# The second MLP projection as seven block products over the whole contraction instead of chunked eighths

## Chip, cores, metric

One NeuronCore of one Trainium2 chip. The metric is device time in microseconds of one execution; three runs of the kernel before gave a median of 2840.08 us (2839.7 to 2841.68). TensorE is written PE, VectorE DVE, ScalarE ACT, GpSimd POOL, SyncE SP. TensorE's clock has two levels, 1.2 and 2.4 GHz; the profile shows the granted share of the higher one.

## What is computed

One inference step of a trunk of two layers with width 1024, for 1024 prompt tokens and 8 sample tokens together (1032 columns, in the order 512 prompt, 8 sample, 512 prompt). Each layer is a token mixer and a squared-ReLU MLP; only the MLP's second half and what borders on it are touched:

```
x = x + g1 * out                                  # token mixer
h = rmsnorm(x, norm_mlp[l]) * (1.0 + s2) + sh2
x = x + g2 * (jnp.square(jax.nn.relu(h @ mlp_w1[l])) @ mlp_w2[l])
...
y = rmsnorm(x, norm_final)
```

`mlp_w1` is 1024 x 4096, `mlp_w2` is 4096 x 1024. The results have to hold float32 accuracy.

## The kernel before, in words

Everything is feature-major: a tile has 128 features in the partitions and tokens along the free dimension. TensorE works in `fp32r`, so each operand is split into a high and a low part (ACT casts `hi`, DVE subtracts to get `lo`), and `mm3` (lines 422 to 430) issues three matmuls for each pair of operands: hi·hi (L425), hi·lo (L428), lo·hi (L429).

A weight unit is a tile of 128 x 1024. `prep` (L377) makes one: a transfer on the SP queue into `raw` (two buffers), the ACT cast into `whi`, the DVE subtraction into `wlo` (three buffers each). `need` keeps units prepared up to three ahead of the one in use (`AHEAD = 3`) and takes one step of `ada_gen` (L258), which in layer 0 computes the next layer's modulation during the second projection: each step issues four transfers of 256 KB for the step after (`t<-ada`) and a group of small matmuls (L287) on the transfers of the step before. The 4 PSUM buffers `pd` of two banks each, 8 temporaries `t2` and 8 `t3` are shared by all of this.

`mlp` (L700) has two halves.

*First projection.* The 4096 x 1024 product is already done in seven half-size block products (Strassen-Winograd form): for each of 16 pairs p of row tiles (`NPAIR`), the products 1, 6, 7, 5, 2, 4, 3 of 24 matmuls with 258 columns each (`AOPS`). The two token halves have 516 columns (`HX`). DVE combines the products, and four of the seven steps finish a tile: `ff_out` (L708) applies ReLU and square on ACT, splits into hi and lo (ACT cast L616, DVE subtraction L617) and stores both parts to DRAM (`fd`) on the POOL queue. The products 1 and 2 of the last two pairs are computed early (`FRONT[1]`, before pair 12) and kept in DRAM, and right there the first chunk of the second projection's operand starts to be loaded (`load_ff(0)`).

*Second projection.* Plain: the contraction of 4096 in 8 chunks of 4 row tiles (`NCH`, `load_ff`: 8 transfers `ffc<-fd` of 516 KB a chunk on the POOL queue). For each of the 8 output row tiles m and 3 token blocks (256, 264 and 512 columns) `out_tile` (L553) accumulates 12 matmuls and DVE adds the gated result into the residual `x` (L544; L547 collects the 8 sample columns). The last chunk goes block by block (`out_last`), and the norm that follows (next layer's, or the final one) runs behind its blocks; the final norm ends the kernel with the writes of `o_y` (L1794).

The order on each engine is set by a scheduler from the written order; transfers issued by `dma_aux` (POOL) keep the written order, those by `dma` (SP) may be moved.

## Time and profile before

| | |
|---|---|
| median of 3 runs | 2840.08 us |
| the profiled execution, device time | 2840.66 us |
| its span, first to last instruction | 2838.9 us |
| mean granted clock | 0.983 |
| second projection, layer 0 | about 889 to 1279 us, the `ada` steps of layer 1 in it |
| second projection, layer 1 | about 2455 to 2827 us |
| first projection, layer 0 / layer 1 | about 540 to 889 / 2120 to 2455 us |

Busy time of an engine is a share of the span; a matmul's own duration includes its passage through the array and overlaps the next one's, so the pace of TensorE is read from the distance between starts. "Idle before, releaser" names what ended an engine's wait.

### The profile page before, as it was taken

The page shows a single profiled execution, that of the slowest core. Times are in us where ns is not written, and L with a number is a line of the kernel's source. Part 1 is how long each engine was busy: PE and PEld are TensorE (multiplying, and loading weights), DVE is VectorE, ACT ScalarE, POOL GpSimd, SP SyncE. Part 2 cuts the span into 40 slices and gives each one's busy share as a digit, 9 for nine tenths or more (in the row PEclk, how much of TensorE's full clock was granted, in tenths as well). Part 3 has the DMA queues.
Part 4 walks back from the last instruction along what each step waited for, and adds up shares of the span by engine and source line. Part 5 has one row for each costly group of instructions (what it writes and reads, how often), then busy time and mean ns, then how long its engine had stood idle before and what let it go on. Part 6 is the DMA issues. An engine that isn't in the chain of part 4 may idle for free. (4 is left out here: it accounts for less than half of the span.)

```text
span 2838.9 us, 47163 instructions
## 1 busy us (share of the span) xinstructions
PE 2726.7 (96%) x18644; PEld 2444.6 (86%) x18644; DVE 1851.9 (65%) x3723; ACT 1390.4 (49%) x2351; POOL 223.2 (8%) x384
## 2 busy tenths in 40 slices
PE   6999999989999999999899999999999999999997
PEld 4889888889998888888789897787789999899996
DVE  5666444797665333357788888998779767544446
ACT  5775411565563000027686766878667556300102
POOL 0000000121113101000000000000002111300100
PEclk8999999999999999999999999999999999999999
DMA  8332333366459666514645545543436654944431
GB/s 297 81 100 65 102 119 120 101 201 206 143 155 347 233 215 235 186 53 87 160 143 131 182 127 141 148 130 112 116 123 190 205 163 142 331 153 143 164 109 63
DMA packets 193581, 441.60 MB, mean 156 GB/s; under 512 B 31377, under 2 KB 49169, under 8 KB 193361
## 3 DMA queue, kind: packets, MB, share of 16 engines
q1 hardware_dynamic: 129808, 269.25, 31.9%
q0 software_dynamic: 63552, 169.34, 18.0%
q8 instruction: 147, 2.41, 0.4%
q14 instruction: 74, 0.60, 0.1%
HBM read 340.44 MB, written 98.08 MB: 154 GB/s over the span
## 5 line engine op out<-in xcount | busy, mean ns | idle before, releaser
L407 ACT CAST whi<-raw 128x1024 fp32r<-128x1024 f32 x220 | 229.9, 1046 | 820.4 <-PE pd L428 584.6
L425 PE MATMUL pg<-hh,whi 128*128 128x256 f32 (+2 forms) x1616 | 537.6, 333 | 11.1 <-ACT hh L525 5.7
L428 PE MATMUL pg<-hl,whi 128*128 128x256 f32 (+2 forms) x1616 | 525.2, 325 | 1.9 <-DVE hl L526 1.9
L429 PE MATMUL pg<-hh,wlo 128*128 128x256 f32 (+2 forms) x1616 | 524.3, 324 | 0.0
L425 PE MATMUL pd<-ffc,whi 128*128 128x256 f32 (+2 forms) x1488 | 479.2, 322 | 3.3 <-DVE x L544 2.4
L544 DVE SCALAR_TENSOR_TENSOR x<-pd,mod,x 128x256 f32<-128x256 f32 (+1 forms) x384 | 219.2, 572 | 399.7 <-PE pd L429 395.0
L429 PE MATMUL pd<-ffc,wlo 128*128 128x256 f32 (+2 forms) x1488 | 477.4, 321 | 0.0
L428 PE MATMUL pd<-ffc,whi 128*128 128x256 f32 (+2 forms) x1488 | 476.2, 320 | 0.0
L408 DVE TENSOR_TENSOR wlo<-raw,whi 128x1024 fp32r<-128x1024 f32 x220 | 269.0, 1224 | 160.1 <-ACT whi L407 149.2
L425 PEld LDWEIGHTS pg<-hh,whi 128*128 128x128 f32 x1616 | 310.0, 192 | 48.7 <-issue 7.6
L428 PEld LDWEIGHTS pg<-hl,whi 128*128 128x128 f32 x1616 | 310.3, 192 | 31.0 <-issue 5.5
L429 PEld LDWEIGHTS pg<-hh,wlo 128*128 128x128 f32 x1616 | 309.5, 192 | 24.5 <-issue 0.7
L425 PEld LDWEIGHTS pd<-ffc,whi 128*128 128x128 f32 x1488 | 280.4, 188 | 44.0 <-ACT whi L407 15.9
L425 PE MATMUL pd<-hh,whi 128*128 128x258 f32 x1024 | 294.1, 287 | 15.8 <-ACT t L781 4.4
L429 PEld LDWEIGHTS pd<-ffc,wlo 128*128 128x128 f32 x1488 | 279.9, 188 | 22.6
L428 PEld LDWEIGHTS pd<-ffc,whi 128*128 128x128 f32 x1488 | 279.9, 188 | 21.8 <-issue 0.2
L428 PE MATMUL pd<-hh,whi 128*128 128x258 f32 x1024 | 292.1, 285 | 0.7 <-DVE hh L617 0.7
L429 PE MATMUL pd<-hh,wlo 128*128 128x258 f32 x1024 | 290.5, 284 | 0.0
L425 PEld LDWEIGHTS pd<-hh,whi 128*128 128x128 f32 x1024 | 196.2, 192 | 19.5 <-issue 6.1
L428 PEld LDWEIGHTS pd<-hh,whi 128*128 128x128 f32 x1024 | 195.9, 191 | 1.8 <-DVE hh L617 1.3
L429 PEld LDWEIGHTS pd<-hh,wlo 128*128 128x128 f32 x1024 | 196.0, 191 | 0.0
L425 PE MATMUL pg<-ffh,whi 128*128 128x264 f32 (+2 forms) x544 | 176.9, 325 | 1.1 <-ACT bcz L1478 0.7
(319 smaller groups left out, 5458.5 us busy)
## 6 DMA issues: line engine op xcount, KB each, us to landing
raw<-W SPq DMA_DIRECT2D x307, 512.0 KB, 4.2
ffc<-fd POOLq DMA_DIRECT2D x128, 516.0 KB, 11.2
fd<-x POOLq DMA_DIRECT2D x100, 516.0 KB, 4.4
t<-ada SPq DMA_DIRECT2D x192, 256.0 KB, 5.5
t<-csd SPq DMA_DIRECT2D x64, 256.0 KB, 4.7
fd<-t POOLq DMA_DIRECT2D x56, 258.0 KB, 4.6
x<-xd POOLq DMA_DIRECT2D x16, 516.0 KB, 10.6
t<-st_ss SPq DMA_DIRECT2D x32, 256.0 KB, 4.4
```

The costliest lines, as they stand in the source:

```text
L407: S.copy(hi, raw)
L408: V.tensor_sub(lo, raw, hi.bitcast(F32))
L425: mm = PE.matmul(pt, wh, xh, start=first and i == 0, stop=False)
L428: PE.matmul(pt, wh, xl, start=False, stop=False)
L429: PE.matmul(pt, wl, xh, start=False, stop=last and i == n - 1)
L544: V.scalar_tensor_tensor(x[:, m, s:s + npr], pt[:, :npr], mod[:, self.gi + m, 0:1], x[:, m, s:s + npr], op0=ALU.mult, op1=ALU.add)
```

## The change

The second projection is done in seven half-size products too, over the whole contraction: outputs in two halves of 4 row tiles (m = 0 to 3), contraction in two halves, tokens in two halves of 516. The four blocks of the squared-ReLU activations are B11, B12, B21, B22, and T1 = B12 - B11, T3 = B22 - B12, T2 = T3 + B11, T4 = B21 - T2. Products in the order 2, 1, 5, 6, 7, 3, 4, with the right operands B21, B11, T1, T2, T3, B22, T4.

- **First projection**: `ff_out` no longer splits. ACT squares into one of 8 slots in the upper half of tile `X`; DVE forms T3, T2, T1 and T4 there; seven tiles of 258 KB a pair are stored in float32 (`td`) where there were four pairs of hi and lo.
- **Right operands**: `load_op` loads half an operand (8 row tiles, four transfers, 2.1 MB) into the `lo` tile and splits it in place, in four pieces of 2 x 516 columns (`split_op`), into three sets of buffers that take turns. The first half operand is loaded at the old place of `load_ff(0)`, the second before the last product of pair 15.
- **Weights**: products 2, 1 and 4 use units as stored. Products 5, 6 and 7, 3 need sums: for each of their 8 units two transfers of 256 KB bring the first summand (a unit, or the sum stored earlier), one of 512 KB the second, DVE adds or subtracts (2 x 512 columns), and the sums of 5 and 6 are stored to DRAM (`sd`) two units later for 6 and 3.
- **Products**: a unit serves 2 output row tiles x 4 contraction tiles x 2 column halves x 3 = 48 matmuls of 258 columns; 8 units a product. Product 4 runs in two column halves of 8 units with 24 matmuls each, and so loads its units twice. A product's result is added to one to four tiles of `x` (`BOUT`: 1, 4, 2, 3, 2, 1, 1 for 2, 1, 5, 6, 7, 3, 4).
- The residual `x` is two tiles of 4 rows (`Two`), reloaded at once; the sample columns are kept aside (`xs`) and added before the last column half of product 4. The following norm is spread by hand over products 3 and 4 (`to_odd`, `to_out`); its last block has 258 columns (before: 256).

```diff
+BPROD = (2, 1, 5, 6, 7, 3, 4)
+BOPS = [(i, hb, q, mp) for i in range(7) for hb in (range(2) if i == 6 else (None,))
+        for q, mp in (BSEQ if i else BFIRST)]
+BSET = [(0, 1), (2, 0), (1, 2), (0, 1), (2, 0), (1, 2), (0, 1)]
...
+            while sums and sums[0][0] <= idx - 2:
+                _, d, h = sums.pop(0)
+                for j in range(2):
+                    dma(d[:, 512 * j:512 * j + 512], h[j])
+            pr = BPROD[i]
+            if pr in (5, 6, 7, 3):
...
+                h = [t2(512), t3(512)]
+                for j in range(2):
+                    dma(h[j], a[:, 512 * j:512 * j + 512])
+                raw = load_unit(*second)
+                for j in range(2):
...
+                        V.tensor_sub(h[j], h[j], raw[:, c])
+                    S.copy(hi[:, c], h[j])
+                    V.tensor_sub(lo[:, c], h[j], hi[:, c].bitcast(F32))
...
-                hi, lo = (M["X"][:, k, i * HX:i * HX + HX] for i in range(2))
-                split_to(hi, lo, r)
-                dma_aux(fd[m][:, :, half * HX:half * HX + HX], v2(M["X"][:, k]))
+            d = slot(p, i)
+            S.activation(d, r, AF.Square)
+            if q != 2:
+                store({5: "B21", 4: "B22", 3: "B11"}[q], p, d)
+            if q == 4:
+                V.tensor_sub(slot(p, 3), d, slot(p, 1))
+                store("T3", p, slot(p, 3))
+            elif q == 3:
+                t1, t2_, t4 = slot(p, 1), slot(p, 5), slot(p, 6)
+                V.tensor_add(t2_, slot(p, 3), d)
+                V.tensor_sub(t1, t1, d)
+                V.tensor_sub(t4, slot(p, 0), t2_)
...
+            for c in range(0, KT, 2):
+                dma_aux(lo[:, c:c + 2].bitcast(F32), d[:, c:c + 2])
...
-                        for b in range(3):
-                            out_tile(ws(m), srcs, res, m, b)
-                            bg.tick()
+            for m in (2 * mp, 2 * mp + 1):
+                if q == qs[0]:
+                    pts[m] = pd()
+                pt = pts[m]
+                for b in range(2) if hb is None else (hb,):
+                    c = slice(b * hw, b * hw + hw)
+                    mm3(pt[:, b, 0:hw], [(hi[:, o:o + P], lo[:, o:o + P], rh[:, k, c], rl[:, k, c])
+                                         for k, o in ((q % 2 * 4 + k, 256 * k + m % 2 * P) for k in range(4))],
+                        q == qs[0], q == qs[-1])
+                if q == qs[-1]:
+                    for o, th in BOUT[BPROD[i]]:
...
+                            V.scalar_tensor_tensor(xv, pt[:, :, 0:hw], gate, xv, op0=ALU.mult, op1=ALU.add)
```

The SP queue during the second projection of layer 0, where the `ada` transfers run (`raw<-W` is a weight unit, `t` are temporaries). Before:

```order
L202 DMA raw<-W 128x1024
L202 DMA t_11825<-ada 128x512
L202 DMA t_11826<-ada 128x512
L202 DMA t_11827<-ada 128x512
L202 DMA raw<-W 128x1024
L202 DMA t_11828<-ada 128x512
L202 DMA t_11930<-ada 128x512
L202 DMA t_11929<-ada 128x512
L202 DMA t_11931<-ada 128x512
```

Four `ada` transfers stand between two weight units, and each of those units feeds 72 matmuls. With the change, in product 6:

```order
L217 DMA sd<-t_10680 128x512
L217 DMA sd<-t_10681 128x512
L217 DMA t_10850<-sd 128x512
L217 DMA t_10851<-sd 128x512
L217 DMA raw<-W 128x1024
L217 DMA t_10921<-ada 128x512
L217 DMA t_10922<-ada 128x512
L217 DMA t_10923<-ada 128x512
L217 DMA t_10924<-ada 128x512
L217 DMA sd<-t_10757 128x512
L217 DMA sd<-t_10758 128x512
```

Now nine transfers go with each unit, and a unit feeds 48 matmuls; the sums stored here are those of two units earlier.

DVE in the second projection of layer 0. Before, with L544 the addition into `x`, L547 the sample columns and L408 the split of a weight unit:

```order
L408 TENSOR_TENSOR wlo<-raw,whi 128x1024
L544 SCALAR_TENSOR_TENSOR x<-pd,mod,x 128x256 x2
L547 TENSOR_TENSOR racc<-pd,racc 128x8
L544 SCALAR_TENSOR_TENSOR x<-pd,mod,x 128x512
L544 SCALAR_TENSOR_TENSOR x<-pd,mod,x 128x256 x2
L547 TENSOR_TENSOR racc<-pd,racc 128x8
L544 SCALAR_TENSOR_TENSOR x<-pd,mod,x 128x512
```

With the change, at the end of product 6 and in product 7 (L452 forms a weight sum, L454 splits it, L837 splits a piece of the right operand, L953 adds into `x`):

```order
L452 TENSOR_TENSOR t_11260<-t_11260,raw 128x512
L452 TENSOR_TENSOR t_11261<-t_11261,raw 128x512
L837 TENSOR_TENSOR rr<-rr 128x2x516
L454 TENSOR_TENSOR wlo<-t_11260,whi 128x512
L454 TENSOR_TENSOR wlo<-t_11261,whi 128x512
L837 TENSOR_TENSOR rr<-rr 128x2x516 x3
L953 SCALAR_TENSOR_TENSOR x<-pd,mod,x 128x516
L452 TENSOR_TENSOR t_11344<-t_11344,raw 128x512
L452 TENSOR_TENSOR t_11345<-t_11345,raw 128x512
L960 TENSOR_TENSOR racc<-pd,racc 128x4
```

Four operations a unit where there was one, and additions into `x` queue behind operations that need a transfer (`raw`).

The POOL queue at the end of layer 1's first projection, with the change (pairs 13 to 15; `b_` and `kept` are tiles of pairs 14 and 15 put aside earlier):

```order
L223 DMA td<-x 128x516 x7
L223 DMA t_25691<-kept 128x516
L223 DMA x<-b_25115 128x516
L223 DMA td<-x 128x516 x7
L223 DMA x<-b_25181 128x516
L223 DMA td<-x 128x516 x3
L223 DMA rr<-td 128x2x516 x4
L223 DMA td<-x 128x516 x4
L223 DMA x<-xd 128x1032 x8
```

The eight loads of the residual and the half operand of product 1 that follow them start only when the last four tiles of pair 15 have been stored.

## Rows read from the trace of the kernel before

**Rows 1.** The page's busy times of the engines over the span.

```profile
PE 2726.7 (96%) x18644; PEld 2444.6 (86%) x18644; DVE 1851.9 (65%) x3723; ACT 1390.4 (49%) x2351; POOL 223.2 (8%) x384
```

**Rows 2.** Stretches of 50 us: the stretch and its length, busy us (and instructions) of PE, weight loads (PEld), DVE, ACT and POOL, granted clock, busy share of the DMA engines, GB/s. The first two lie in layer 1's first projection, the third in the mixer before it, the last two in layer 1's second projection.

```profile
2250.00:2300.00 50.00, 50.00 (x420) 50.00 (x419) 36.88 (x61) 27.37 (x46) 7.89 (x12) 1.00 0.60 181
2300.00:2350.00 50.00, 50.00 (x418) 49.80 (x417) 33.57 (x54) 27.50 (x47) 6.06 (x9) 1.00 0.43 130
...
1850.00:1900.00 50.00, 50.00 (x254) 40.92 (x253) 47.70 (x97) 37.98 (x59) 1.43 (x2) 1.00 0.37 120
...
2500.00:2550.00 50.00, 50.00 (x319) 45.10 (x318) 21.09 (x41) 5.27 (x5) 2.09 (x5) 1.00 0.17 48
2600.00:2650.00 50.00, 50.00 (x317) 45.01 (x316) 19.92 (x39) 4.34 (x5) 5.90 (x12) 1.00 0.49 166
```

**Rows 3.** The PE timeline, start and duration in us: two neighbouring matmuls of 512 and of 256 columns in the second projection, and of 258 in the first.

```profile
2601.67 0.40 PE L425 MATMUL pd<-ffc,whi 128*128 128x512 f32 x1
2601.91 0.40 PE L428 MATMUL pd<-ffc,whi 128*128 128x512 f32 x1
...
2604.48 0.28 PE L425 MATMUL pd<-ffc,whi 128*128 128x256 f32 x1
2604.60 0.28 PE L428 MATMUL pd<-ffc,whi 128*128 128x256 f32 x1
...
745.18 0.28 PE L425 MATMUL pd<-hh,whi 128*128 128x258 f32 x1
745.30 0.28 PE L428 MATMUL pd<-hh,whi 128*128 128x258 f32 x1
```

**Rows 4.** The chain of work that ended last, start and duration: the same matmul of a 512-column group in two successive output row tiles (36 matmuls apart).

```profile
2467.15 0.24 PE pd L428
2472.83 0.24 PE pd L428
```

**Rows 5.** Groups by line, engine, operation and shape (count, busy us, mean ns, idle before): layer 1's second projection (the first four), its first projection (the others).

```profile
L544 DVE SCALAR_TENSOR_TENSOR x<-pd,mod,x 128x512 f32<-128x512 f32 x64 | 48.1, 751 | 130.4 <-PE pd L429 130.4
L408 DVE TENSOR_TENSOR wlo<-raw,whi 128x1024 fp32r<-128x1024 f32 x28 | 34.3, 1225 | 2.9
L407 ACT CAST whi<-raw 128x1024 fp32r<-128x1024 f32 x28 | 29.5, 1055 | 279.6 <-PE pd L428 279.6
L547 DVE TENSOR_TENSOR racc<-pd,racc 128x8 f32<-128x8 f32 x56 | 8.7, 156 | 0.0
...
L403 DVE TENSOR_TENSOR wlo<-t,whi 128x512 fp32r<-128x512 f32 x44 | 29.2, 686 | 0.0
L617 DVE TENSOR_TENSOR x<-t,x 128x516 fp32r<-128x516 f32 x40 | 27.8, 695 | 24.7 <-ACT x L616 24.7
L616 ACT CAST x<-t 128x516 fp32r<-128x516 f32 x41 | 25.6, 625 | 1.3
```

**Rows 6.** Stretches around the place where the first chunk of the second projection's operand is loaded, in layer 0 and layer 1, and one in the first chunks of layer 0's second projection (columns as in the stretches above).

```profile
860.00:880.00 20.00, 15.98 (x107) 15.39 (x106) 11.98 (x19) 8.49 (x15) 4.80 (x8) 0.83 1.06 349
2430.00:2445.00 15.00, 11.05 (x65) 10.37 (x64) 9.40 (x15) 5.76 (x10) 3.43 (x6) 0.77 1.16 378
...
870.00:875.00 5.00, 3.75 (x17) 3.55 (x18) 4.71 (x8) 4.10 (x7) 0.54 (x1) 0.61 1.27 387
900.00:905.00 5.00, 5.00 (x35) 4.58 (x34) 1.98 (x2) 1.06 (x1) 1.12 (x3) 1.00 1.14 387
910.00:915.00 5.00, 5.00 (x33) 4.45 (x32) 2.23 (x5) 1.05 (x1) 1.44 (x3) 1.00 1.04 414
```

**Rows 7.** DMA issues by line (count, KB each, median us from issue to landing): two from layer 1's second projection (2500 to 2750 us), two from 850 to 885 us, one from 900 to 965 us, where the DMA engines are full.

```profile
raw<-W SPq DMA_DIRECT2D x22, 512.0 KB, 3.8
ffc<-fd POOLq DMA_DIRECT2D x40, 516.0 KB, 9.4
...
fd<-x POOLq DMA_DIRECT2D x6, 516.0 KB, 11.0
raw<-W SPq DMA_DIRECT2D x4, 512.0 KB, 6.4
...
raw<-W SPq DMA_DIRECT2D x6, 512.0 KB, 10.5
```

**Rows 8.** The PE timeline in layer 0's second projection: one `ada` step (8 records in one row) and the matmul after it.

```profile
1010.07 1.06 PE L287 MATMUL pd<-t,ct 128*32 128x512 f32 x8
1011.06 0.39 PE L425 MATMUL pd<-ffc,whi 128*128 128x256 f32 x1
```

**Rows 9.** The end of the kernel: a stretch with the last output tiles and the norm behind them, the last matmul of the projection, the norm's own matmul, and the last multiplications by the norm on DVE.

```profile
2797.00:2827.00 30.00, 25.71 (x198) 24.18 (x196) 24.71 (x73) 10.59 (x24) 0.00 (x0) 1.00 0.25 93
...
2826.61 0.28 PE L429 MATMUL pd<-ffc,wx 128*128 128x256 f32 x1
2828.96 0.70 PE L461 MATMUL pd<-t,ones 128*128 128x256 f32 x2 [2.07 <-DVE t L493]
...
2832.30 2.07 DVE L1794 SCALAR_TENSOR_TENSOR x<-x,nf,t 128x256 f32<-128x256 f32 x5
```

More of the change, by code (lines that the diff above doesn't have):

```diff
@@ L824, in mlp @@
+            bg.tick(2)
+        x = new_x()
+        for m in range(KT):
+            dma_aux(x[:, m, :], xd[:, m])
+        load_op(1, 0)
+        acc = tp.tile([P, KT, NS], F32, name="racc", tag="racc", bufs=2)
+        V.memset(acc, 0.0)
+        fin = finish()
+        pts = {}
+        hw = HX // 2
+        for n, (i, hb, q, mp) in enumerate(BOPS):
+            j = n % 8
+            hi, lo = need(f"b{l}", n)
+            if n == 8 and more:
                 ada[0] = more()
-            elif c == NCH - 1:
+            elif i == 6 and hb == 0 and j == 0:
```

331 lines of the change are left out of this document (227 added, 104 removed).

## Prediction, made before the changed kernel ran

> **What bounds the kernel now.** Read the busy times first [rows 1]: PE is busy for 96% of the span, DVE for 65%. Since a PE record overlaps the next, the second look is at stretches of 50 us [rows 2]: in both projections of layer 1 PE never stops, with DVE at 20 to 37 of 50 us, the granted clock at 1.00 and the DMA engines at 0.17 to 0.60. So the two projections run at the pace of the matmuls, and the third look is at what sets that pace. Two starts of 512 columns lie 0.24 us apart, two of 256 or 258 columns 0.12 us [rows 3]. Half the columns, half the time: the price goes by columns and hardly by the matmul. Averaged over many: an output row tile of 36 matmuls (12 each of 256, 264 and 512 columns) repeats after 5.68 us [rows 4], and 838 matmuls of 258 columns took 100 us [rows 2], 0.1193 us each.
>
> **The sum** is made against the profiled execution, 2840.66 us (span 2838.9 and 1.8 around it), 0.6 above the median of the three runs. About 0.2%, 5.7 us, is what a measurement can tell from no change.
>
> *1. Matmuls.* Before, a layer's second projection is 8 chunks x 8 output row tiles = 64 groups of 5.68 us [rows 4]: 363.5 us. After, 7 products x 8 units x 48 = 2688 matmuls of 258 columns, where there were 2304 wider ones: 2688 x 0.1193 = 320.7 us [rows 2]. More instructions, fewer columns: 42.8 us less a layer, **-85.6 us** in both. The `ada` steps of layer 0, 24 of about 1.0 us [rows 8], stay.
>
> *2. First projection.* Each pair loses four ACT casts of 0.625 us and four DVE subtractions of 0.695 us and gets four DVE operations of the same width [rows 5]. PE is full there while ACT has 27 and DVE 37 of 50 us [rows 2]: 0. Cover gone would mean DVE at 50 of 50.
>
> *3. The burst before pair 12.* Before, 4.2 MB of operand are loaded between the stores there, at 349 to 378 GB/s, and PE loses time: 107 matmuls in 20 us and 65 in 15 us [rows 6], where the steady pace gives 8.4 a us, so 168 and 126 [rows 2]. That is 61 x 0.1193 = 7.3 us in each layer, partly because the clock falls to 0.61 after the pause [rows 6], a mixture of 1.2 and 2.4 GHz. The change loads 2.1 MB there. I take half of the loss back: **-7 us** (0 to -14.5).
>
> *4. Start of the second projection.* The first four units of product 2 need only the half operand loaded early, and last 4 x 48 x 0.1193 = 22.9 us. In that time come the second half (2.1 MB), the residual (4.2 MB) and half an operand of product 1 (2.1 MB): 8.4 MB at about 400 GB/s [rows 6] is 21 us, but the residual waits for the last stores of pair 15. Before, a similar load was borne at a full PE, in the stretches from 900 us [rows 6]. **+3 us** (0 to +10).
>
> *5. Products 5 and 6 in layer 0.* This is the place I trust least. A unit keeps PE for 48 x 0.1193 + 1.0 = 6.7 us, and asks for 1.05 MB of `ada`, 0.52 MB of first summand, 0.52 MB of second, 0.52 MB of sum to store, and its eighth of the right operand, 0.53 MB: 3.15 MB. The full DMA engines moved 387 to 414 GB/s [rows 6], so 3.15 MB take 7.6 to 8.1 us: the transfers, not PE, set the pace. There is also a chain on SP: an `ada` transfer needs a temporary whose sum was stored one unit before, so SP stands until that store has landed, and the next unit's loads stand behind it. I take 8.0 us a unit: 16 x 1.3 = 20 us, less about 6 for the one unit that weights are ahead, plus 3 for clock falls like those at the burst [rows 6]: **+17 us**. Below: 0, if fewer transfers coincide. Above: 10.5 us a unit, the landing time of a weight unit when the engines are full [rows 7], which gives 16 x 3.8 = 60 us.
> The Trainium skill, "DMA: Bandwidth & Descriptors", section "Where 436 GB/s comes from", says that for transfers between HBM and SBUF the HBM side binds at about 358 GB/s for a core. By that figure a unit would take an estimated 8.8 us and the term would be about 30 us; the rows here show 387 to 414 GB/s over 5 us and up, so I stay with the rows.
>
> *6. Products 5 and 6 in layer 1* have no `ada`: 2.10 MB a unit, 5.2 us at 400 GB/s against 5.73 us of PE. Just hidden; weight sums can be formed up to five units ahead there. **+3 us** (0 to +10). DVE is closest to full in product 6: 16 tile-wide sums (8 units of 2 adds) and 16 splits at 0.69, 8 operand splits at 1.24 (by width from L408), 12 additions into `x` at 0.75 and 12 small ones at 0.16 come to 42.9 of 45.8 us [rows 5]. The mixer shows DVE at 47.70 of 50 us under a full PE [rows 2], so I price that at 0; without that cover it would be queued behind `raw`.
>
> *7. Product 4* takes 16 units of 24 matmuls, 2.86 us each. A `raw` buffer is held for landing 3.8 us [rows 7], cast 1.05 and subtraction 1.23 [rows 5], 6.1 us; two buffers give a unit every 3.05 us at best. 16 x 0.2 = 3 us are late. In layer 1 the final norm comes on top: DVE sums to about 46 of 45.8 us, and before, such a stretch with DVE at 24.71 of 30 us held PE at 25.71 [rows 9]. **+3 and +6 us** (0 to +8 each).
>
> *8. The end.* From the last matmul at 2826.6 us over the last addition, square, norm matmul and eight multiplications to the end is 12.2 us [rows 9]; the last block now has 258 columns instead of 256 and the same steps: 0 (2 either way).
>
> Sum: 2840.7 - 85.6 - 7 + 3 + 17 + 3 + 9 = **2780 us**, 2.1% faster.
>
> **The rivals.**
> *A. All transfers hide.* Terms 5 and 6 vanish and the burst's loss comes back wholly: 2780 - 20 - 7.5 = 2752 us. For it: the layer 1 engines have room [rows 2], and 8 + 8 temporaries let loads run ahead. Against: 3.15 MB in 6.7 us is more than any row moved.
> *B. Layer 0 runs at landing time,* 10.5 us a unit: +60 instead of +17, 2823 us. For it: stores of 11.0 us and weight units of 10.5 us in full stretches [rows 7], and nine transfers a unit on one queue. Against: those medians belong to queues that were filled by far more than a unit's transfers.
> *C. Slower: the store-to-load chain paces products 5 and 6 in both layers.* If the round trip of a sum (stored, landed, its buffer refilled, the next unit's summand landed) is 10.5 us in layer 1 as well [rows 7], the terms 5 and 6 become 16 x 3.8 + 16 x 4.8 = 136 us instead of 20: 2896 us. It decides from the point where 16 x (T - 6.7) + 16 x (T - 5.73) eats the 80.6 us that the other terms leave, at T = 8.7 us a unit in both layers. Against: in layer 1 the SP queue waits for no `ada`, and 2.1 MB in 8.7 us is 241 GB/s, which the engines exceed easily; stores and loads of neighbouring units are independent.
> *D. The pace goes by weight load, not by column.* There is one weight load a matmul, and in the first projection PEld is busy 50.00 of 50.00 us [rows 2]. Were the 0.12 us the load's, the 384 additional matmuls a layer would cost 2 x 384 x 0.119 = 91 us instead of saving: 2932 us. Against: in the second projection, with half the matmuls at 512 columns costing 0.24 us [rows 3], PEld has gaps (45 of 50) [rows 2] and PE none, so columns bind.
> The Trainium skill's page "TensorE: Matmul & The Clock Gate", section "Back-to-back issue gap", gives for sustained pairs of load and matmul about 81 ns at 128 columns and 131 ns at 512, so that wide matmuls are much cheaper a column; by it, as an estimate, the change would be about 12 us slower a layer. The rows show 0.24 us at 512 columns, twice that at 256, so this case does not bear it out.
>
> **How the numbers follow.** Forecast (2765 to 2800): 0.60. A: 0.18. B, and between it and the forecast: 0.13. C, any mixture that passes its point: 0.05. D: 0.01. Stalls that just cancel the gain: 0.03. Faster 0.60 + 0.18 + 0.13 = 0.91; same 0.03; slower 0.06. The range reaches from A's time to B's: 2752 to 2823; C, D, the cancelling case and a part of A's lower side lie outside, under 0.2.
>
> **What would show it.** Term 1: matmuls of 258 columns at 0.119 us, a product without stalls in 45.8 us, a second projection of layer 1 near 330 us where it was 372. Term 3: the stretch before pair 12 with more than 107 matmuls in 20 us. Term 5: units of about 8 us in products 5 and 6 of layer 0, PE waiting for `ada` or for a weight sum, DMA share at 1 and above 380 GB/s. Term 6: PE full in the same products of layer 1. Term 7: PE with gaps of a few tenths in product 4, ended by the cast or the subtraction. It is wrong if PE stalls in products 1, 2 or 3, if layer 1's products 5 and 6 stall as much as layer 0's, or if DVE, not DMA, ends the waits.

## The result, and the profile of the changed kernel

The changed kernel takes 2819.57 us (median of four runs, 2814.00 to 2825.63), the kernel before on the same chip 2839.89: ratio 0.9928, 95% interval 0.9907 to 0.9950. The profiled execution took 2820.48 us (span 2818.7). The interval is clear of 1, and the gain is 0.7%. The forecast was 2780: the sign held, the size did not. Of 60 us forecast, 20 came.

The page's busy times, which answer to [rows 1], its two rows on the splits of the operand, and its two rows on the DMA issues that matter below:

```profile
PE 2662.7 (94%) x19442; PEld 2453.6 (87%) x19442; DVE 1995.6 (71%) x3800; ACT 1496.6 (53%) x2477; POOL 277.9 (10%) x476
...
L836 ACT CAST rr<-rr 128x1032 fp32r<-128x1032 f32 x112 | 117.3, 1056 | 156.5 <-DMA rr<-td 156.4
L837 DVE TENSOR_TENSOR rr<-rr 128x1032 fp32r<-128x1032 f32 x112 | 135.5, 1227 | 64.4 <-ACT rr L836 64.1
...
raw<-W SPq DMA_DIRECT2D x371, 512.0 KB, 4.3
...
rr<-td POOLq DMA_DIRECT2D x112, 516.0 KB, 8.4
```

PE was busy for 96% and is for 94% of a shorter span: it now waits. ScalarE stands 156 us before the operand's splits, for the operand to land; whether that costs anything is looked at below.

Stretches of the changed kernel (columns as in [rows 2]): layer 0's products 5 and 6, then in layer 1 the end of product 2, product 5, the border from product 6 to 7, and the end:

```profile
990.00:1050.00 60.00, 54.71 (x444) 48.05 (x444) 37.08 (x66) 17.38 (x25) 6.99 (x11) 1.00 1.01 368
1050.00:1110.00 60.00, 56.62 (x448) 49.52 (x441) 34.99 (x58) 15.84 (x23) 3.67 (x7) 0.97 1.03 390
...
2455.00:2505.00 50.00, 46.77 (x366) 46.35 (x365) 27.46 (x32) 20.55 (x21) 17.50 (x28) 0.93 0.91 340
...
2550.00:2590.00 40.00, 40.00 (x337) 40.00 (x336) 32.47 (x57) 12.77 (x20) 3.10 (x5) 1.00 0.97 340
...
2640.00:2670.00 30.00, 21.94 (x153) 21.53 (x152) 19.48 (x33) 10.71 (x15) 2.82 (x4) 0.83 0.72 256
...
2777.00:2807.00 30.00, 28.07 (x208) 28.02 (x209) 15.39 (x34) 10.46 (x22) 0.00 (x0) 0.89 0.42 125
```

Product 5 of layer 1 runs full: the 337 matmuls in its 40 us include those cut by the ends of the stretch, and by the starts a unit of 48 takes 5.75 us, 0.1198 us each. At the border to product 7 it is 153 in 30 us where some 250 would fit.

By stages (from the first to the last matmul of each): first projections 347.1 -> 344.6 and 335.1 -> 342.8 us, second projections 396.0 -> 383.8 and 371.0 -> 358.5, the mixer between them 835.7 in both, the end 12.3 -> 11.5. (Layer 0's second projection of before ends at 1285 us, not at 1279 as the table of stages has it.) So each second projection won 12 us where the matmuls alone give 42.8.

What a product takes beyond its matmuls (45.8 us), beyond the busy time of `ada`'s and, in product 4, beyond that of the norm's own products (L520, 1.0 to 2.7 us), from the starts of every 48th matmul (24th in product 4), in us. The 1.0 of product 1 in layer 0 is `ada`'s too: its steps are busy for 1.07 us each, but lengthen a unit by 1.2 us, from 5.75 to 6.94.

```
                   layer 0                             layer 1
product         2    1    5    6    7    3    4     2    1    5    6    7    3    4
the change     3.7  1.0  6.8  6.0  4.1  0.2 12.9   6.7  0.2  0.2  4.3 12.2  0.2 12.5
late_rstd      2.8  1.0  7.0  6.1  6.1  0.2  5.9   6.5  0.2  0.2  4.9 13.2  0.2  6.5
rawsums        4.8  1.0  1.2  0.9  0.5  0.2 12.8   0.2  0.2  0.2  0.2  0.2  0.2 12.9
quarter_op     4.6  1.0  3.2  0.9  2.1  0.2 11.1   4.8  0.2  2.0  0.2  0.2  0.2 10.7
nostore        3.6  1.0  9.6 10.6  1.9  1.8 12.7   4.1  0.2  0.2  0.2 10.8  0.2 12.6
no_ada         4.1  0.2  0.2  3.6 12.2  0.2 12.3   4.0  0.2  0.2  3.7 13.2  0.2 12.1
late_pin       7.1  1.0  6.1  4.8  1.5  0.2  8.5   9.0  0.2  1.7  8.7  0.2  0.2  6.2
late_paced_pin 7.5  1.0  2.5  7.7  1.0  0.2  8.6   9.2  0.2  0.2  0.8  8.4  0.2  6.2
```

Two places carry most of it: product 4, and the borders of products 5 to 7.

**Product 4.** PE's waits in layer 1's second projection (us in total, times, longest), PE's timeline in layer 0, and the stretch of 10 us around it:

```profile
PE pd L488 <- DVE wlo L454: 10.5, 3, 4.0
PE pd L602 <- ACT sm L599: 4.9, 1, 4.9
PE pd L520 <- DVE t L552: 2.4, 1, 2.4
PE pd L484 <- ACT whi L463: 2.3, 1, 2.3
```

```profile
1241.73 1.45 PE L602 MATMUL pd<-sm,ones 128*128 128x8 f32 x6 [4.93 <-ACT sm L599]
```

```profile
1236.00:1246.00 10.00, 5.07 (x27) 4.86 (x26) 6.01 (x13) 3.36 (x9) 0.00 (x0) 0.67 0.50 159
```

L602 are the sixteen ones products of `sample_rstd`, eight columns wide (the view ends after six). They stand in PE's queue right behind the first half of product 4, and wait for that half's own eviction, gated sum, add to `x` and squares. PE stops 4.9 us, the granted clock of the 10 us around is 0.67 (a mixture of 1.2 and 2.4 GHz), the sixteen products take 3.6 us, and the unit takes 11.4 us where 2.9 are matmuls.

**The border of products 6 and 7.** VectorE in layer 1 (L452 and L450 form weight sums, L454 splits one into `wlo`), ScalarE's cast of product 7's first weight sum, PE where it goes on, and the POOL queue's operand transfers:

```profile
2643.18 1.29 DVE L452 TENSOR_TENSOR t<-t,raw 128x512 f32<-128x512 f32 x2 [6.26 <-issue]
2645.70 1.29 DVE L452 TENSOR_TENSOR t<-t,raw 128x512 f32<-128x512 f32 x2 [1.22 <-DMA raw<-W]
2646.91 1.29 DVE L454 TENSOR_TENSOR wlo<-t,whi 128x512 fp32r<-128x512 f32 x2
2650.01 1.29 DVE L452 TENSOR_TENSOR t<-t,raw 128x512 f32<-128x512 f32 x2 [1.82 <-issue]
2655.60 0.69 DVE L450 TENSOR_TENSOR t<-raw,t 128x512 f32<-128x512 f32 x1 [4.29 <-DMA t<-sd]
```

```profile
2631.72 1.14 ACT L453 CAST whi<-t 128x512 fp32r<-128x512 f32 x2 [4.62 <-PE pd L487]
```

```profile
2647.64 0.58 PE L488 MATMUL pd<-rr,wlo 128*128 128x258 f32 x1 [4.04 <-DVE wlo L454]
```

```profile
2631.99 2.82 POOL L223 DMA_DIRECT2D rr<-td  x4 [35.71 <-PE pd L488]
2643.56 2.11 POOL L223 DMA_DIRECT2D rr<-td  x3 [8.76 <-PE pd L488]
```

The landing time of a weight tile issued right behind the first burst, at 2635.75 us:

```profile
DMA to landing us min/median/max: 9.8/9.8/9.8
```

Both half operands of a product, 2.1 MB each, go out within 15 us (the view ends at the third transfer of the second). The weight tile issued behind the first takes 9.8 us to land, where the page's median is 4.3. VectorE stands 6.26 us before a sum (the trace names no releaser; the sum's `raw`, issued at 2634.54, has no landing on record) and 1.22 us before the next, for the tile above. Counted from the first unit of product 5, two sums, two casts and two splits a unit, these are the sums of product 7's units 5 and 6, needed 29 us later and more. Behind them in VectorE's queue stands the split of product 7's first unit, whose cast was done at 2632.9: PE stops 4.0 us for it. The second unit's split, cast by 2641.3, starts at 2659.1, behind the sum at 2655.60, which belongs to product 3 and waits 4.3 us for a stored sum. So what stops PE is not that its own weights land late, but that VectorE's queue holds a sum for a unit far ahead, whose transfer is late, in front of the split that PE needs next. PE's three waits of this kind come to 10.5 us (L454 above); after the first the matmuls start 0.21 us apart for 4 us, with a granted clock of 0.57 from 2645 to 2650 us.

In layer 0's products 5 to 7 PE waits for evictions and for `ada`'s loads; below, VectorE and PE at the border from product 5 to 6:

```profile
PE pd L484 <- DVE racc L960: 8.8, 4, 3.2
PE pd L316 <- DMA t<-ada: 3.0, 4, 1.9
```

```profile
1054.79 1.29 DVE L452 TENSOR_TENSOR t<-t,raw 128x512 f32<-128x512 f32 x2 [2.75 <-DMA raw<-W]
1056.00 0.15 DVE L960 TENSOR_TENSOR racc<-pd,racc 128x4 f32<-128x4 f32 x1
```

```profile
1057.03 0.36 PE L484 MATMUL pd<-rr,whi 128*128 128x258 f32 x1 [3.15 <-DVE racc L960]
```

In this longest of the four, too, a sum that waits for `raw` stands in VectorE's queue ahead of what PE needs, here the eviction that frees a PSUM buffer.

### The profile page after: what moved, and what is told of

The parts are those of the page before. It is cut to its first block, busy times and chain, and to the rows that moved or that the text cites. A ratio compares the mean times of both kernels' runs of the same rounds, so it can differ in the third digit from the quotient of the medians.

```text
span 2818.7 us, 49673 instructions
## 1 busy us (share of the span) xinstructions
PE 2662.7 (94%) x19442; PEld 2453.6 (87%) x19442; DVE 1995.6 (71%) x3800; ACT 1496.6 (53%) x2477; POOL 277.9 (10%) x476
## 5 line engine op out<-in xcount | busy, mean ns | idle before, releaser
L484 PE MATMUL pd<-rr,whi 128*128 128x258 f32 x1792 | 516.3, 288 | 11.7 <-DVE racc L960 8.8
L488 PE MATMUL pd<-rr,wlo 128*128 128x258 f32 x1792 | 512.4, 286 | 13.4 <-DVE wlo L454 10.5
L487 PE MATMUL pd<-rr,whi 128*128 128x258 f32 x1792 | 511.2, 285 | 0.0
L484 PEld LDWEIGHTS pd<-rr,whi 128*128 128x128 f32 x1792 | 344.5, 192 | 32.1 <-issue 26.0
L488 PEld LDWEIGHTS pd<-rr,wlo 128*128 128x128 f32 x1792 | 344.4, 192 | 16.3 <-DVE wlo L454 11.1
L487 PEld LDWEIGHTS pd<-rr,whi 128*128 128x128 f32 x1792 | 344.2, 192 | 0.5 <-issue 0.5
L484 PE MATMUL pd<-hh,whi 128*128 128x258 f32 x1024 | 294.9, 288 | 21.6 <-ACT whi L424 10.6
L836 ACT CAST rr<-rr 128x1032 fp32r<-128x1032 f32 x112 | 117.3, 1056 | 156.5 <-DMA rr<-td 156.4
L837 DVE TENSOR_TENSOR rr<-rr 128x1032 fp32r<-128x1032 f32 x112 | 135.5, 1227 | 64.4 <-ACT rr L836 64.1
```

The lines of the kernel that those rows point to most:

```text
L484: mm = PE.matmul(pt, wh, xh, start=first and i == 0, stop=False)
L487: PE.matmul(pt, wh, xl, start=False, stop=False)
L488: PE.matmul(pt, wl, xh, start=False, stop=last and i == n - 1)
L836: S.copy(hi[:, c:c + 2], src)
L837: V.tensor_sub(lo[:, c:c + 2], src, hi[:, c:c + 2].bitcast(F32))
```

## The experiments

Chips differ (before ran at 2836 to 2856 us beside these), so ratios to before are compared; the change has 0.9928.

**late_rstd.** The samples' ones products three units later:

```
-        yield                      (to_odd, ahead of sample_rstd)
+        yield  x4
-        r8 = sample_rstd(sm(NS))   (to_out: moved into the writes of n1, m == 1; the rows ys at m == 2)
```


> The squares' sum of the samples (the ones products of sample_rstd) is formed three units later, in the second half of product 4, in both layers; nothing else moves. Theory: in the profile of the change PE stands 5.1 us in each layer before those ones products (the two gaps put down to ACT sm L599), because they stand in PE's queue behind the last unit of the first half and wait for that unit's own eviction, the gated sum, the add to x and the squares. With the clock fall after it the last unit of the first half took 11.4 and 9.7 us where 2.9 are matmuls, and the next one 5.0 and 6.4. Both units then fall below 5 us, and 10 to 16 us come back in all: about 2807 us. Rival 1: the stop only moves with the products (the chain behind them is late there too): a gap of 4 to 5 us in the second half of product 4, and 2816 to 2822 us. Rival 2: it is won in product 4 and lost again where the samples' columns are then late (start of the odd mixer, output of the samples): the second projection shortens and the stretch after it grows by as much.


Measured 2802.95 us, 0.9888 (0.9870 to 0.9905): the last unit of the first half takes 2.9 us in both layers (11.4 and 9.7), the lost time in product 4 goes from 12.9 and 12.5 to 5.9 and 6.5. The theory holds for the place, and of PE's waits the one for L602 is gone. The trace has 9 us of the gain in the second projections; the rest lies in stages that the edit does not touch, and in which traces of different runs differ by as much.

**late_norms.** The other ones products of product 4 later too:

```
+yield  x2      (ahead of nm.rstd in to_odd and of n0.rstd in to_out)
+yield          (ahead of n1.rstd in to_out; the writes of the output bunched by two)
```


> late_rstd, and the ones products of the other norms that stand in PE's queue during product 4 later as well: those of the 512 columns two units later in both layers, those of the 254 columns in layer 1 one unit later; the writes of the output are bunched by two to end in the same unit. Theory: they too wait in PE's queue for evictions, squares and adds that are only just done (in late_rstd the second unit of product 4 took 7.8 and 8.2 us, and three units of the second half 4.5 to 4.6, where 2.9 are matmuls): 4 to 5 us of each layer's first half and 3 us of layer 1's second half come back beyond late_rstd, about 2792 us. Rival: the chain of squares and adds on ScalarE and VectorE is itself behind, so the wait only moves on with the products: 2799 to 2804 us.


Measured 0.9885 (0.9869 to 0.9901), no more than late_rstd. The wait of the first half went (0.0 and 1.4 us lost there), but the second half now loses 3.5 and 4.9: most of it moved on, as the rival has it.

**spread_op, spread_both, late_spread2.** The transfers of the operands one in a unit:

```
-    dma_aux(lo[:, c:c + 2].bitcast(F32), d[:, c:c + 2])
+    later.append((lo[:, c:c + 2].bitcast(F32), d[:, c:c + 2]))
+    if later: dma_aux(*later.pop(0))                  (at the end of each unit)
```


> The first half operand of a later product (load_op(i + 2, 0)) still begins to load after the last unit of a product, but its four transfers of 516 KB go out one in a unit over four units instead of four at once; each is still loaded two units or more before it is split. Theory: the stops at the borders of the products come from the two half operands, eight transfers of 516 KB in 11.5 us on the POOL queue, which fill the DMA engines while raw<-W and t<-sd wait behind them (9.7 to 9.8 us to landing at 2634 to 2637 us of the change's profile). In layer 1 products 6 and 7 took 50.1 and 58.0 us where 45.8 are matmuls, in layer 0 the first units of products 5, 6 and 7 took 9.4, 12.0 and 10.3. By this 10 to 16 us of layer 1 and 5 to 10 us of layer 0 come back: about 2800 us, and the landing of raw<-W in that stretch falls to 5 us or less. Rival: the weight sums are late by their own chain (DVE in program order, SP's queue, two raw buffers), whatever else is on the DMA engines: units 0 and 1 of product 7 in layer 1 stay over 9 us, and the time within 4 us of 2820.

> Both half operands of a product go out spread, one transfer of 516 KB in each unit: the one that was issued at once after unit 5 in units 5, 6, 7 and 0, the one after unit 7 in units 1 to 4 of the next product, each split later by a unit where its load moved. In spread_op only the second burst was spread. Theory: in layer 1 raw<-W and t<-W that were issued at 2635.75 to 2637.1 us, right behind the first burst (2632.0 to 2634.1), landed after 9.7 to 9.8 us with the DMA engines full, and the sums of the next two units were late by that; a weight tile then never stands behind more than one operand transfer and lands in 6 us or less. Products 6 and 7 lose 5 us or less together in layer 1 (16.5 in the change) and products 5 to 7 8 us or less in layer 0 (17): 18 to 22 us, 0.986 of before. Rival: the same bytes in the same product keep the DMA engines full whatever the order, or the sums' chain on VectorE is late anyhow; the first two units of product 7 keep over 16 us together, and the ratio stays at 0.991 to 0.994.

> late_rstd and spread_both together. Theory: the two lie in different products (4 there, 5 to 7 here), so their gains add: 0.9888 times what spread_both gives against the change's 0.9928, 0.982 if that is 0.986. Rival: what the first gives back is taken by the second (the odd mixer or the output then waits for something else): no better than the better of the two.


Measured 0.9934 (0.9920 to 0.9949), 0.9963 (0.9950 to 0.9976), 0.9901 (0.9886 to 0.9916): none is faster than its counterpart without the edit. They say nothing on the burst, since it was still there. POOL in spread_both:

```profile
2637.47 2.83 POOL L223 DMA_DIRECT2D rr<-td  x4 [35.19 <-PE pd L488]
```

Four in 2.8 us, as in the change, although the program has them in four different units: POOL's queue waits once, for the last matmul on the buffer, and then sends all four, so a later place in the program changes nothing.

**rawsums, quarter_op, nostore.** Three kernels that leave transfers out, and so do not compute the whole reference.

```
rawsums:     both terms of a sum from the one raw tile; no dma(h[j], ...), no store of sums
quarter_op:  dma_aux(lo[:, 0:2]...) alone; src = lo[:, 0:2] for all four parts
nostore:     a = A["W"][...] also in products 6 and 3; sums.append(...) left out
```


> In products 5, 6, 7 and 3 the two terms of each weight sum are taken from the one raw tile that is loaded anyway, so the transfers of the first term, the stores of the sums of products 5 and 6 and their loads in 7 and 3 are left out (what is summed is then not what the kernel needs); VectorE and ScalarE do the same work. Theory: what is lost in these products (17 us over the matmuls in layer 0, 16.5 in layer 1) is lost to transfers, three of 256 KB beside each 512 KB of weights: 25 to 33 us come back, about 2790 us, and products 5, 6, 7 and 3 take 45.8 to 48 us each (in layer 0 with 7 to 8 of ada matmuls more). Rival (VectorE's own queue): the adds, subtractions and evictions are the pace; then products 6 and 7 of layer 1 keep 50 and 58 us and the time stays over 2812.

> Of each half operand only the first of four transfers is made, and all four parts are split from it (the operands are then not those the kernel needs); every other instruction stays, the transfers of the weight sums too. Theory: the stops at the product borders need the operands' bursts, 2.1 MB each; at a quarter of that products 6 and 7 of layer 1 take 46 to 48 us each (50.1 and 58.0) and layer 0's products 5 to 7 lose 5 us or less (17), product 2's last units too: 26 to 35 us, 0.981 to 0.984 of before. Rival: the extra load per unit of the sums and its wait on SP and VectorE make the stops, as nostore left open; then over 8 us stay at the border of products 6 and 7, and the ratio over 0.989.

> The sums of products 5 and 6 are not stored, and products 6 and 3 load a weight tile where they loaded a stored sum (the sums are then not those the kernel needs). The loads into half tiles, VectorE's and ScalarE's work and SP's order of loads stay; a unit of products 5 and 6 moves 1.0 MB in place of 1.5. Theory (how much moves in a row): products 6 and 7 of layer 1 fall to 46 to 48 us (50.1 and 58.0 now), and layer 0's 5 to 7 lose 3 to 9 us in place of 17: 20 to 27 us, about 2796 us. Rival (the extra load and its wait in SP's queue and on VectorE): the stops at the border of products 6 and 7 stay at over 8 us in both layers, 2810 us or more.


Measured 2777.63 us, 0.9793 (0.9778 to 0.9808); 2785.35 us, 0.9793 (0.9776 to 0.9810); 0.9929 (0.9914 to 0.9944). Products 6 and 7 of layer 1 in the change, in rawsums and in quarter_op:

```profile
2592.00:2702.00 110.00, 99.48 (x786) 98.86 (x785) 76.30 (x126) 37.32 (x55) 11.69 (x17) 0.94 0.79 283
```

```profile
2560.00:2655.00 95.00, 95.00 (x795) 95.00 (x794) 78.40 (x129) 39.10 (x55) 12.24 (x18) 1.00 0.54 186
```

```profile
2567.00:2662.00 95.00, 95.00 (x796) 95.00 (x795) 76.57 (x127) 35.52 (x52) 3.56 (x5) 1.00 0.68 233
```

With most of the operand's bytes or with the sums' transfers away PE is full, with VectorE busy for 77 to 78 of 95 us: the amount of VectorE's work is not the pace. Without the stores alone most of the loss stays (in layer 1's products 6 and 7 10.8 us of 16.5, all in product 7; in layer 0's products 5 to 7 22 us where it was 17), although they are a third of a unit's weight bytes in products 5 and 6. So what counts is not bytes alone, but that loads which a sum waits for are late.

**no_ada.**

```
-mlp(0, mi(0, 5), to_odd, more=lambda: ada_gen(1, ...))
+V.memset(mod[:, 48:96], 0.25); mlp(0, mi(0, 5), to_odd)
```


> The modulation of layer 1 is not computed in the second projection of layer 0 but set to a constant: its matmuls (24.4 us of TensorE by the rows of before), its 6 MB a group of loads and the PSUM tile that it holds are left out. Theory: in layer 0 the held PSUM tile and its loads cost more than the matmuls: the stops that end with an eviction (racc L960, 9.5 us in products 5 to 7) go, so 30 to 40 us come off and layer 0's products 5 to 7 look as layer 1's: about 2785 us. Rival: ada costs only its matmuls, and the stops at the borders of the products stay: 24 us, 2796 us, with the first units of products 5, 6 and 7 still over 9 us.


Measured 2787.96 us, 0.9823 (0.9805 to 0.9841); layer 0's second projection is 29.3 us shorter than the change's, of which 28.6 are `ada`'s 24 steps of 1.19 us. Layer 0 then looks as layer 1 does (3.6 and 12.2 us lost in products 6 and 7), and PE's waits in these products now end with the split L454 (10.7 us), no longer with evictions. Products 5 to 7 lose 16.0 us without `ada`, 16.9 with it: the loss moved, from 12.8 us in products 5 and 6 to 3.8 there and 12.2 in product 7. So the rival, by the sum: `ada` costs its matmuls, and without it stops of the same size come in another place.

**order251.**

```
-BPROD = (2, 1, 5, 6, 7, 3, 4)
+BPROD = (2, 5, 1, 6, 7, 3, 4)
```


> One line: the products of the second projection run in the order 2, 5, 1, 6, 7, 3, 4 (before 2, 1, 5, 6, 7, 3, 4), so that product 1, whose units load 512 KB, stands between 5 and 6, whose units move three times that (raw, the other term or a sum, and the store of a sum). Theory after spread_op and rawsums: what stops products 6 and 7 is the transfers that 5 and 6 need in a row, 1.5 MB in 5.75 us beside the operands' 4.2 MB in 46 us, some 360 GB/s for 92 us, which uses up what the weights were ahead; split by a light product it does not build up. In layer 1 the 4.3 and 12.2 us lost in products 6 and 7 fall to 4 or less together, in layer 0 the 17 lost in 5, 6 and 7 to 8 to 12: 17 to 21 us, about 2800 us. Rival: it is the chain of a sum itself (stored in 5, loaded in 6, stored in 6, loaded in 3; SP's queue in order) and not how much moves: the first two units of product 7 keep over 20 us together, and the time stays over 2812.


Measured 0.9934 (0.9921 to 0.9947). Neither forecast: the stops moved. 13.8 us in layer 0 and 7.3 in layer 1 are lost in product 5, now second; in layer 1 5.9 us stay in product 7. Setting a light product between 5 and 6 does not take the loss away.

**raw3.**

```
-N2, N3E, N3O, N3M = 8, 14, 6, 8
+N2, N3E, N3O, N3M = 8, 14, 6, 6
+if ph.nr % 3 == 0: pool, tag, n = ph.pool, "rawx", 1       (load_unit, in the MLPs)
```


> In both MLPs a third raw tile of weights; to make room, six t3 tiles in place of eight. Theory: the stops in the first projection (7.3 us in layer 1 at 2158, 2213, 2243 and 2275 us, about as much in layer 0, and 5.5 us in each before pair 12) come from the loop of two raw tiles: a load starts when the tile before last has been summed, and takes 4.7 us and up to 6.3. With a third one 8 to 12 us come back in the first projections, and the second projections lose less at the borders: about 2805 us. Rival: with the loads earlier the same bytes only collide earlier (the DMA engines are at 0.6 of their time there and full in the bursts), or the t3 tiles that were given up stop the sums: within 4 us of 2820, or slower.


Measured 0.9930 (0.9917 to 0.9942). Layer 1's first projection took 334.4 us (342.8), layer 0's 346.7 (344.6); layer 1's products 6, 7 and 3 lost 24 us (16.7 in the change). One edit with two sides, in no place clear; a third raw tile did not take the stops away.

**paced, late_paced, late_paced_fp, paced1, late_paced1.** Ahead of each operand transfer GpSimd copies one column of a weight tile, so that POOL's queue cannot run ahead:

```
+ nc.gpsimd.tensor_copy(pace[:, 0:1], units[wpos[0] + 2][1][:, 0:1])    (paced1: + 1)
  dma_aux(*later.pop(0))
```


> spread_both, and ahead of each operand transfer one column of the weight tile that was split last is copied on GpSimd, so that POOL's queue sends the transfer only when that tile is there: one transfer of 516 KB per unit, behind the weights of the units ahead. Theory (burst): raw<-W and t<-W never stand behind more than one operand transfer, land in 6 us or less in products 5 to 7, and 2 to 6 us are lost there in layer 1 (16.5 in the change) and 4 to 10 in layer 0 (17): 18 us or more less than the change, 0.984 to 0.987 of before. Rival (sum of bytes: 2.0 MB in 5.75 us in products 5 and 6 is what the DMA engines move at best): the stops stay over 10 us in each layer, wherever they fall, or operands come late as new stops at units 2 and 3: 0.990 to 0.996.

> late_rstd and paced together. Theory: the gains lie in different products and add: about 0.9888 times paced's ratio over 0.9928, 0.981 if paced gives 0.985. Rival: no better than the better of the two.

> late_paced, and the first half operand of product 2, whose four transfers go out at once before pair 12 in the first projection, paced too: one in every two products of pair 12. Theory: that burst is what stops TensorE before pair 12 (5.45 us at 862.1 and 5.51 at 2423.6 us in the change, after ScalarE's split of a weight tile that landed late): the stop falls below 2 us in both layers, and 7 to 10 us come back beyond late_paced. Rival: the stop is made by the sixteen weight rows of pairs 14 and 15 themselves, which need one load per product where others need none: it stays within 1 us of 5.5, as before the change too.

> paced, each operand transfer gated by the weight tile of one unit earlier, so that it goes out some 5.75 us sooner: in paced the split of the operand on ScalarE waited for the transfer 154 us in 27 places of layer 1, one unit's time each, and the weights' splits stood behind it. Theory (burst): these waits go to under 1 us each, raw<-W still lands in 8 us or less, and products 5 to 7 lose 4 to 8 us in each layer where the change loses 17: 0.985 to 0.988 of before. Rival (sum of bytes): with the waits of paced gone the stops at the borders are back as in the change: over 12 us in each layer, 0.991 to 0.996; third case: the gates and the operands are still in each other's way, slower than before.

> late_rstd and paced1 together. Theory: the gains add, 0.996 times the ratio of paced1, so 0.981 to 0.984 if the burst is the cause; rival: no better than late_rstd's 0.9888.


Measured 1.0377 (1.0358 to 1.0396), 1.0336 (1.0320 to 1.0351), 1.0338 (1.0324 to 1.0352), 1.0321 (1.0304 to 1.0338), 1.0283 (1.0269 to 1.0298): all slower, the third case of paced1. The first two waits of `paced` from 2560 to 2800 us (`pace` is the gate), then ScalarE's waits in products 5 to 7 of paced1's layer 1, and of the change's:

```profile
ACT rr L839 <- DMA rr<-td: 154.2, 27, 10.9
POOL pace L977 <- DVE wlo L454: 152.7, 22, 10.0
```

```profile
ACT rr L839 <- DMA rr<-td: 134.6, 25, 8.7
```

```profile
ACT whi L453 <- PE pd L487: 51.2, 11, 8.3
ACT rr L836 <- DMA rr<-td: 37.6, 19, 6.3
```

ScalarE's queue holds the splits of operands ahead of weights' splits, in an order made by the scheduler and not written in the code. A gate then waits for a weight split that stands behind the split of an operand not yet sent, and so the transfers come late: in paced1 they go out 8 us apart on the average from 2615 to 2657 us, where a unit's matmuls take 5.75. The last row shows that in the change, too, ScalarE stands 38 us there for operands, with weights' splits behind it. But none of PE's stops there ends with a cast (all three end with VectorE's L454), so in the change this wait is not what stops PE.

In late_paced_fp the gates in the first projection held nothing: the four transfers went out at 852.50, 853.34, 854.74 and 856.69 us, and each gate took 0.2 us without a wait.

**late_pin and late_paced_pin.** The splits of both kinds held in the written order, without and with paced1's gates, both with late_rstd's edit:

```
-S.copy(hi[:, c:c + 2], src)
+tc.keep_in_program_order(S.copy(hi[:, c:c + 2], src))      (and each sum and split of prep and load_op)
```


> late_rstd, with the splits of weights and operands in the second projection held in the order in which the code writes them on ScalarE and VectorE (the sums of a unit's two halves ahead of their splits). Theory: the order changes what waits for what a little, not the bytes: products 6 and 7 of layer 1 together still lose 12 to 20 us and the ratio is that of late_rstd, 0.987 to 0.991. Rival: the order in which the scheduler bunched the operands' splits is itself the cause of the stops: under 8 us lost there, 0.984 or less.

> late_pin with paced1's transfers: one operand transfer per unit, gated by a weight tile, and the splits in an order in which no gate stands behind the split that waits for it. Theory (burst): products 5 to 7 lose 4 to 8 us in each layer (16 to 19 in late_rstd), ScalarE waits under 20 us in all for operands in layer 1, 0.981 to 0.985. Rival (sum of bytes, two raw tiles): over 12 us are lost in each layer although the longest landing of raw<-W is under 8 us, 0.987 or more. Third case: the gates still delay the operands, slower than late_pin.


Measured on one chip: 2830.93 us, 0.9914 (0.9898 to 0.9929), and 2817.48, 0.9865 (0.9850 to 0.9880). ScalarE's waits in the same products of late_pin:

```profile
ACT whi L458 <- PE pd L494: 41.9, 13, 4.6
ACT whi L458 <- DVE t L455: 31.0, 6, 8.7
ACT whi L458 <- DVE t L451: 19.9, 5, 6.2
```

PE's waits in late_pin there:

```profile
PE pd L491 <- ACT rr L843: 4.4, 1, 4.4
PE pd L494 <- DVE rr L844: 1.8, 2, 0.9
```

ScalarE has no wait for an operand left, and PE none for a weight's split or an eviction; in late_rstd its waits for the split L454 came to 12.4 us there. So the order did make those stops. In their place PE waits for the operand's own splits (L843, L844; in layer 0 one of 3.4 us). Products 5 to 7 lose 12.4 and 10.6 us (19.2 and 18.3 in late_rstd), between the forecasts of theory and rival. But product 2 loses 4.3 and 2.5 more, and as a whole late_pin is not faster than late_rstd.

late_paced_pin beats late_pin by 13 us by the medians, with intervals apart, and against late_paced1, which has the same gates without the fixed order, it is 4.1% lower. It also has spread_both's later loads and splits of a half operand, so the 13 us are those of gate and spread together. Its own forecasts both missed: 11.2 and 9.4 us are lost in products 5 to 7, and the longest landing of a weight tile in layer 1's is 9.1 us (11.0 in late_pin). The profiled runs show only 1.2 us less than late_pin in products 5 to 7 of each layer; they were late_pin's fastest and late_paced_pin's slowest, so where the rest lies stays open. late_paced_pin has the lowest ratio of all kernels that compute the whole reference; against late_rstd, on another chip, the intervals overlap.

## Why the prediction was wrong

The step that failed first is in term 6: VectorE was priced at 0 because its busy time fits (42.9 of 45.8 us), and product 7 got no term at all. What counts is not how busy VectorE is but what stands in its queue: sums that wait for a late `raw` in front of the splits that PE needs. Product 7 lost 12.2 us in layer 1. By terms:

1. *Matmuls: right.* Products without a stop take 46.0 us (1, 5 and 3 of layer 1), 0.1198 us a matmul; the 0.1193 of the sum came from counts that include matmuls cut by the ends of a stretch, worth 1.3 us a layer. Rival D is refuted. Of the miss of 40 us some 3 are here.
2. *First projection, 0:* -2.5 and +7.7 us with term 3. Layer 1's took 337 to 344 us in all kernels with this projection but raw3 and quarter_op, and none of them came down to before's 335.1. PE's waits there, up to 2.0 us and 7.5 in all from 2105 to 2300 us (4.0 in as long a stretch of before), end mostly with VectorE's combination of products (L890) and with casts of weights (L424). VectorE itself waits 30.7 us for `raw` there, 20.7 before.
3. *The burst before pair 12, -7: failed.* PE stops 5.3 us before 867.6 and 5.4 before 2429.2 us. The stretch in the change and in quarter_op:

```profile
855.00:875.00 20.00, 14.71 (x112) 14.54 (x111) 15.39 (x23) 8.98 (x15) 6.42 (x12) 0.91 0.94 328
```

```profile
850.00:870.00 20.00, 19.87 (x165) 19.61 (x165) 17.06 (x25) 11.94 (x18) 6.27 (x12) 1.00 0.88 322
```

   112 matmuls in 20 us where 168 fit, so 6.7 us are lost; before it was 107 and 7.3 [rows 6]. I halved the loss because the bytes were halved. With a quarter of the operand it is gone, at nearly the same GB/s. late_paced_fp, where 4.6 and 5.1 us stayed, tests nothing here, since its transfers were hardly spread. The trace of the change shows a chain that the sum did not have. VectorE, ScalarE and PE:

```profile
857.28 1.23 DVE L837 TENSOR_TENSOR rr<-rr 128x1032 fp32r<-128x1032 f32 x1 [0.49 <-ACT rr L836]
858.43 0.68 DVE L403 TENSOR_TENSOR t<-raw,t 128x512 f32<-128x512 f32 x1
```

```profile
864.17 0.62 ACT L424 CAST whi<-raw 128x512 fp32r<-128x512 f32 x1 [2.37 <-DMA raw<-W]
```

```profile
867.63 0.55 PE L484 MATMUL pd<-hh,whi 128*128 128x258 f32 x1 [5.29 <-ACT whi L424]
```

   The last weight tile had landed at 854.25, but the sum L403, for which the next load waits, starts only behind the operand splits L837, which waited for their transfers; that load goes out right after it, at 859.15, lands at 864.1, and PE goes on at 867.6. Layer 1 has the same order. The operand splits are new there: the loss of before went, and another of its size came. This is read from the trace; no run tests it by itself.
4. *Start, +3: mis-sized.* Product 2 loses 3.7 and 6.7 us, 10.4 in both layers, mostly in its last units.
5. *Products 5 and 6 in layer 0, +17: near in size (12.8), which is in part luck.* The units without a stop run at 6.9 us, PE's pace with `ada`, not at 8.0, and the loss falls on the borders. The two products moved 22.4 and 22.9 MB, 2.8 MB a unit, not 3.15: `ada` has 13 steps there, not 16. The engines were full, as the term has it, at 368 and 390 GB/s over 60 us each, but without `ada` the stops only move on to product 7. The Trainium skill, "DMA: Bandwidth & Descriptors", section "Where 436 GB/s comes from", has the HBM side bind at about 358 GB/s for a core; here 390 were moved over 60 us, so for this core the measurement decides against it.
6. *Products 5 and 6 in layer 1, +3:* 4.5. *Product 7 had no term, and lost 12.2 us in layer 1 and 4.1 in layer 0.* I averaged a unit's bytes over its time, and VectorE's work over a product's. My own condition, "without that cover it would be queued behind `raw`", is what happened, with VectorE only 70% busy: 4.2 MB of operand in two bursts at a border make `raw` late, and the sum that waits for it holds up splits and evictions. That sums can be formed five units ahead, which the term counts in its favour, is what put them in front.
7. *Product 4, +3 and +6: wrong mechanism.* 12.9 and 12.5 us were lost; 7.0 and 6.0 of them went with the samples' ones products (late_rstd). No term looked at what else stands in PE's queue.
8. *The end:* 0 forecast, -0.8.

Ledger: first projections and burst +5 where -7 was forecast, 12 us; second projections -25 where -54 was, 29 us; the end gives 1 back: the 40 us. The products of the change lose 71 us by the table, 39 more than the 32 of terms 4 to 7; some 10 of these before lost too (layer 1's second projection took 371.0 us where its matmuls are 363.5), which the sum did not count. Of what would show me wrong, two came true: PE stalls in product 2, and in layer 1 its waits end with DVE. Layer 1's products 5 and 6 do not stall as layer 0's do (4.5 us against 12.8); only over products 5 to 7 are the two alike (16.7 and 16.9).

Settled: that half of the loss in product 4 is the samples' ones products in PE's queue; that the stops of products 5 to 7 need both the operand's transfers and the sums' loads; that in the change they come from the order of sums and splits, since the waits for a weight's split and for an eviction go when it is fixed (late_pin fixes it on both engines; the trace puts the stops on VectorE); that neither `ada`, the stores nor the amount of VectorE's work makes them. Open: why the fixed order leaves 12.4 and 10.6 us there, with operand splits late in place of weight splits; how much the burst alone is worth; product 2's last units; and a run that tests the chain before pair 12.

## What to carry to other kernels

When a stage gets shorter, list every instruction that stands in the bounding engine's queue inside it, small ones too: sixteen products of eight columns cost 6 to 7 us a layer with what followed. Do the same for the engines that feed it: an engine that is 70% busy still stops the others if its queue holds an instruction that waits for a late transfer in front of one that is needed now. So price a transfer by the burst it goes out in and by what is queued behind the instruction that waits for it, not by bytes per unit of time. And look in the trace whether an edit did what it says: a transfer written later in the program is not sent later if its queue waits only for a buffer, and a gate holds nothing if what it reads is long there.

## What the runs showed that was not expected

- A wait for an operand costs nothing where weights are ahead: in rawsums ScalarE stood 30 us before `rr` in layer 1's products 5 to 7, and PE not at all.
- In and behind a burst transfers of every size are late: around that border a 512 KB weight tile landed after 9.8 us, 256 KB parts issued with it after 9.7 to 9.8, and the 516 KB operand parts after 5.7 to 11.3.
- A gate of one column, on GpSimd, which else only issues transfers there, cost 3.6 to 4.4% against the same kernel without it while weights' splits stood behind operands' in ScalarE's queue. With the splits in the written order, gate and spread together gained 0.5%.
